# The second half of the receptance projection, ahead of the recurrence or beside it

## The chip, the cores and the metric

The kernel runs on one core of a Trainium2 chip. The metric is the device time of one execution in microseconds; of the kernel before three were timed.

## What is computed

Two layers of a causal decoder over 512 tokens of 1024 channels, and a final RMSNorm. Layer 0 is a mixture of windowed and differential attention, layer 1 is RWKV-7 time mixing; each is followed by a squared-ReLU MLP of width 4096. The change lies in layer 1, whose core is:

```python
xr, xw, xk, xv, xa, xg = [h + xx * mu[i] for i in range(6)]
r = xr @ w_r
k = xk @ w_k
v = xv @ w_v
...
def step(state, inp):
    r_t, w_t, k_t, v_t, a_t, b_t = inp
    sa = jnp.einsum('bhij,bhj->bhi', state, a_t)
    state = state * w_t[:, :, None, :] + sa[..., None] * b_t[:, :, None, :] + v_t[..., None] * k_t[:, :, None, :]
    return state, jnp.einsum('bhij,bhj->bhi', state, r_t)
```

r is 512 x 1024: 16 heads of 64 columns. It is read only in the recurrence and in the bonus term beside it.

## The kernel before, in words

Every float32 product is made of three products of a rounded part and a rest: weights and activations are split into hi and lo, and hi x hi, hi x lo, lo x hi are summed in PSUM (`mm3`, lines 175 to 178).

**Ahead of the recurrence** `rwkv_layer` (line 594) writes, in program order (lines 766 to 785): the k projection half 0, the decay path, k half 1, the a path, `xr = mix(0, 1)`, `project(W["w_r"], xr, 0, ...)`, then the gate path (`mix(5, 0)`, `g_weights`, `g_first`, `xv = mix(3, 0)`, `g_second`). `project` (line 709) makes 512 of the 1024 output columns with `gemm_group` (line 192): four chunks of weights, each 256 rows by 512 columns (512 KB). `wchunk` (line 162) loads one on the SP queue into `wraw` (three buffers, which the weights of the small paths use as well), ScalarE casts it to `whi` (line 167), VectorE subtracts it into `wlo` (line 169; two buffers each). With it TensorE does four token blocks x 2 row blocks x 3 matmuls of 512 columns into four PSUM banks. After the last chunk `spilled` (line 713) copies each bank by ScalarE (line 719) and sends it to the DRAM tensor `scr_r` on the ACT queue (line 605). The compiler's scheduler may move instructions of this stage past each other on an engine where their data allows.

**The recurrence** works on 16 units, each of 128 tokens and 4 heads (256 columns); units 0 to 7 are columns 0 to 511 (q = 0, 1), units 8 to 15 the others (q = 2, 3). A unit is a list of some hundred steps, each with a due time `AT[...]` counted in slots; unit n starts `PERIOD` = 8 slots after unit n - 1, so about four units are under way at once. All steps are sorted by due time and emitted in that order, and the `InOrder` wrapper (line 112) ties each engine's instructions to that order. What one unit takes is here called a period. A unit's score matmuls (`psc`, slot 7.0 and 7.1) are followed on VectorE by the masked scores `ms`, the rounding levels `lm`, and a chain of small float16 products (`p0` to `p14`) of which each needs a copy or sum (`e0` to `e14`) on ScalarE or VectorE before the next. Line 137 is the wrapper's, so all instructions of the recurrence carry it.

**Beside the recurrence** a generator, `side_work` (line 1438), fills TensorE with projections that have no place of their own: before the change v columns q = 0 and 1, r columns q = 2 and 3, v columns q = 2 and 3, and then parts of the output projection. `beside` (line 1370) makes 256 columns of 512 tokens in 16 pieces; a piece is 2 row blocks x 3 = 6 matmuls of 256 columns. `SIDE[n]` says how many pieces are spread evenly over period n. Their weights come in chunks of 512 rows by 256 columns (512 KB), cast in quarters by ScalarE and subtracted by GpSimd (lines 1352 and 1363). `evac_r` and `evac_v` copy the two finished banks and send them to DRAM on the ACT queue; `evac_v` also makes a mean-free copy on VectorE. Unit n loads its r at slot 8 n - 1.7 (line 874), and its v late, at 8 n + 18.8 (line 1158).

Of the kernel before, what the change touches and what calls it, by code (L numbers as in the profile page):

```python
# [10 lines left out]
F32 = mybir.dt.float32  # L11
# [7 lines left out]
P = 128  # L19
S = 512  # L20
# [49 lines left out]
FIRST = 8  # L70


SIDE = [16, 8, 9, 7, 8, 8, 9, 6, 11, 8, 6, 0, 8, 8, 6, 5, 8, 6, 7]
ORD = ['tensor', 'scalar', 'vector', 'gpsimd']
PERIOD = 8
PHASE = 0.5939277075075091
# [68 lines left out]
class Builder:  # L145
# [448 lines left out]
    def rwkv_layer(self):  # L594
        tc, nc, A = self.tc, self.nc, self.A
        W = {n: A["rwkv_" + n][0] for n in ("w_r", "w_k", "w_v", "w_o", "w0", "w1", "w2", "a0", "a1", "a2", "g1", "g2")}
# [7 lines left out]
        def spill(name, t, b, hf):  # L604
            nc.scalar.dma_start(scr[name][b * P:(b + 1) * P, hf * 512:(hf + 1) * 512], t)

        with ExitStack() as ctx:
# [20 lines left out]
            def mix(i, which, first=False, behind=None):  # L628
                xh, xl = self.xtiles(which)
                for k in range(KT):  # L630
                    if first:
                        nc.vector.scalar_tensor_tensor(self.h[k], self.h[k], self.g_mix[1][:, k:k + 1], rb,
                                                       op0=ALU.mult, op1=ALU.mult)
                        nc.vector.tensor_tensor(xx[k], self.hz[k][:, 1:S + 1], self.h[k], op=ALU.subtract)
                    t = lp.tile([P, S], F32, tag="mt", name=self.nm("mt"), bufs=3)
                    nc.vector.scalar_tensor_tensor(t, xx[k], mu[:, i, k:k + 1], self.h[k], op0=ALU.mult, op1=ALU.add)
                    if behind is not None and k >= XB:
                        with tc.issue_after(behind.ins):
                            nc.scalar.copy(xh[k], t)
                    else:  # L640
                        nc.scalar.copy(xh[k], t)  # L641
                    eng = nc.vector if not first and (XLA >> i & 1) and k % 2 else nc.gpsimd
                    eng.tensor_tensor(xl[k], t, xh[k], op=ALU.subtract)  # L643
                return xh, xl
# [57 lines left out]
            def wa_second(name, s, w):  # L702

                def mm(pb, bs, cs):
                    nc.tensor.matmul(pb, s[0][:, bs], w[1][0][:, cs], start=True, stop=False)
                    nc.tensor.matmul(pb, s[1][:, bs], w[1][1][:, cs], start=False, stop=True)
                blocks(spilled(name, AF.Tanh, 0.5), mm)

            def project(w, x, hf, evac, behind=None):
                self.gemm_group(w, 0, KT, hf * 512, *x, lambda m, ps: evac(m, hf, ps), token_major=True,  # L710
                                chunk=behind and (lambda *a: self.wchunk(*a, behind=behind)))

            def spilled(name, func=AF.Copy, scale=1.0):
                def evac(b, hf, ps):
                    t = lq.tile([P, 512], F32, tag="sp", name=self.nm("sp"), bufs=5)
                    if name == "g":
                        nc.vector.tensor_copy(t, ps)
                    else:
                        nc.scalar.activation(t, ps, func, scale=scale)
                    spill(name, t, b, hf)  # L720
                return evac
# [54 lines left out]
            xr = mix(0, 1)  # L776
            wa_second("a", sa, wa)
            project(W["w_r"], xr, 0, spilled("r"))
            xg = mix(5, 0)
            wg = g_weights()  # L780
            sg = g_first(xg, wg)
            xv = mix(3, 0, behind=self.gact)
# [7 lines left out]
            with ExitStack() as cx:  # L790
# [15 lines left out]
                def t2(name, pool_=wk, shape=(P, CW), dt=F32, bufs=None):  # L806
                    kw = {} if bufs is None else {"bufs": bufs}
                    return pool_.tile(list(shape), dt, tag=name, name=self.nm(name), **kw)
# [19 lines left out]
                nc = self.nc = InOrder(self, ORD)  # L828
# [3 lines left out]
                done = set()  # L832
# [24 lines left out]
                def unit(n):  # L857
                    b, q = units[n]
# [3 lines left out]
                    def at(name):  # L862
                        def add(f):
                            items.append((PERIOD * n + AT[name], f))
                            return f
                        return add


                    @at("load")
                    def _():  # L870
                        assert q < 2 or f"r{q}" in done
                        for t in ("w", "a", "k", "r"):
                            u[t] = t2("l" + t, ld)
                            nc.sync.dma_start(u[t], scr[t][rows, cs])
# [444 lines left out]
                def tokens(name, q, bk):  # L1319
                    return scr[name].rearrange("(m z p) c -> z p m c", z=2, p=P)[bk][:, :, q * CW:(q + 1) * CW]  # L1320

                def evac_r(q):
                    def evac(bk, ps):
                        t = self.tmp.tile([P, S], F32, tag="sq", name=self.nm("sq"))
                        nc.scalar.copy(t, ps)
                        nc.scalar.dma_start(tokens("r", q, bk), t.rearrange("p (m c) -> p m c", m=2))
                    return evac

                def evac_v(q):
                    def evac(bk, ps):  # L1330

# [38 lines left out]
                def beside(x, evac, name):  # L1370

                    pg = None
                    for kk in (0, 4):
                        wh, wl = taken()
                        if pg is None:
                            pg = [bank(p, name="side") for p in ps_g]
                        for m in range(4):
                            bk, ms = m % 2, slice(m * P, (m + 1) * P)
                            dst = pg[bk][:, (m // 2) * CW:(m // 2 + 1) * CW]
                            for k in range(4):  # L1380
                                xh, xl = x[0][kk + k][:, ms], x[1][kk + k][:, ms]
                                product(dst, [(xh, wh[:, k]), (xh, wl[:, k]), (xl, wh[:, k])], kk + k == 0 and m < 2, kk + k == 7)
                                if k % 2:
                                    if kk + k == 7 and m > 1:
                                        evac(bk, pg[bk])
                                        if m == 3:
                                            done.add(name)
                                    yield 0.5


                def project_o(cg, ks, ts, banks=None, last=True):
# [5 lines left out]
                    for k0 in ks:  # L1397
# [5 lines left out]
                        for m in range(4):  # L1403
# [12 lines left out]
                TH = S // 2  # L1416
                early, later = slice(0, TH), slice(TH, S)
                part_o = [None, None]
                order = [(W["w_v"], xv, evac_v, 0), (W["w_v"], xv, evac_v, 1), (W["w_r"], xr, evac_r, 2), (W["w_r"], xr, evac_r, 3),
                         (W["w_v"], xv, evac_v, 2), (W["w_v"], xv, evac_v, 3)]  # L1420
                first_o, whole_o = (0, 2), (0, 2, 4, 6)
                weights = chunks([(w, kk, 4, q * CW, CW) for w, x, e, q in order for kk in (0, 4)]
                                 + [(W["w_o"], k0, 2, cg * 512, 512) for ks in (first_o, whole_o) for cg in range(2) for k0 in ks]
# [3 lines left out]
                def taken():  # L1427
                    while not ready:
                        convert()
                    return ready.pop(0)  # L1430
# [6 lines left out]

                def side_work():
                    for w, x, e, q in order:
                        yield from beside(x, e(q), ("v" if e is evac_v else "r") + str(q))  # L1440
                    for cg in range(2):
                        yield from project_o(cg, first_o, later)
                    for cg in range(2):
                        yield from project_o(cg, whole_o, early)
# [10 lines left out]

                def outputs():

                    assert "v3" in done and "r3" in done and ("o", 7) in done
                    for l, x in zip((oh, ol), self.xtiles(0)):
                        l += x  # L1460
                    for k in range(KT // 2):
                        halves.append(self.xq.tile([P, S], F32, tag=f"xl{k}", name=self.nm("half")))
                        nc.sync.dma_start(halves[k], scr_o[k * P:(k + 1) * P, :])
                    self.h = [self.xq.tile([P, S], F32, tag=f"xh{k}", name=self.nm("h")) for k in range(KT)]
                    for k in range(KT):
                        nc.sync.dma_start(self.h[k], scr_h[k * P:(k + 1) * P, :])
# [9 lines left out]
                items = [i for n in range(NU) for i in unit(n)] + clears  # L1476
                for n, count in enumerate(SIDE):
                    items += [(PERIOD * (n + (i + PHASE) / count), beside_once) for i in range(count)]
# [8 lines left out]
            nc = self.nc = self.nc.nc  # L1487
# [99 lines left out]
```

## Time and profile before

| | us |
|---|---|
| three runs, median (lowest to highest) | 1526.73 (1521.74 to 1526.81) |
| profiled execution, whole | 1525.81 |
| its span, first to last instruction | 1523.9 |
| TensorE busy, share of the span | 1443.8, 95% |
| VectorE busy | 863.7, 57% |
| ScalarE busy | 684.2, 45% |
| GpSimd busy | 352.0, 23% |
| mean granted TensorE clock | 0.976 |

Layer 1's projections and gate lie at 650 to 793 us of the span, the recurrence with its side work at 793 to 1145, the rest of the output projection and the second MLP behind that. Busy shares are averages over stages with different limits. TensorE's matmuls are pipelined and the profile models their ends, so the time from one matmul's start to the next one's is less than the duration shown. A granted clock of 1.00 is 2.4 GHz; 0.50 is 1.2 GHz, and a figure in between is the mean of a stretch at both.

### The profile page before, as it was taken

The numbers are of one execution on the slowest core, as the hardware profiler recorded it, in microseconds if no ns is written. First come the engines' busy times: TensorE is split into PE (matmuls) and PEld (weight loads), VectorE is DVE, ScalarE is ACT, GpSimd is POOL, SyncE is SP. The second block draws the span as 40 slices with busy tenths as digits, with TensorE's granted clock in tenths as the row PEclk, the third lists the DMA queues.
The fourth block names the chain that finished last, engine by engine and source line by source line (L and its number), as shares of the span: only waits on it lengthen the run. The fifth ranks groups of instructions, "written<-read, shape, count | busy, mean of one in ns | idle before, by whom it ended". The sixth has DMA issues, their size and how long they took to land. (4 is left out here: it accounts for less than half of the span.)

```text
span 1523.9 us, 24386 instructions
## 1 busy us (share of the span) xinstructions
PE 1443.8 (95%) x9506; PEld 1172.4 (77%) x9506; DVE 863.7 (57%) x1491; ACT 684.2 (45%) x1394; POOL 352.0 (23%) x364
## 2 busy tenths in 40 slices
PE   7999999999999999969888999989998999999998
PEld 6765866878888888857667788868787888888887
DVE  5343565632335464497876778878866333354543
ACT  4245364432334343236634666666655233343533
POOL 4210200300000010052336455546655000000100
PEclk9999999999999999979989999989999999999999
DMA  5230310433333233324564345444223333333331
GB/s 193 80 90 1 96 57 27 102 104 85 97 97 97 97 124 98 102 64 152 176 192 147 116 139 154 127 143 119 64 95 118 90 97 97 97 97 97 97 97 70
DMA packets 117115, 159.76 MB, mean 105 GB/s; under 512 B 22524, under 2 KB 57892, under 8 KB 117000
## 3 DMA queue, kind: packets, MB, share of 16 engines
q1 hardware_dynamic: 103240, 140.37, 30.8%
q10 hardware_dynamic: 13760, 17.83, 3.5%
q8 instruction: 75, 1.23, 0.3%
q14 instruction: 40, 0.33, 0.1%
HBM read 133.00 MB, written 19.92 MB: 100 GB/s over the span
## 5 line engine op out<-in xcount | busy, mean ns | idle before, releaser
L169 DVE TENSOR_TENSOR wlo<-wraw,whi 128x1024 fp32r<-128x1024 f32 x172 | 219.9, 1280 | 263.1 <-ACT whi L167 263.0
L167 ACT CAST whi<-wraw 128x1024 fp32r<-128x1024 f32 x172 | 180.5, 1050 | 253.0 <-PE g L177 236.2
L176 PE MATMUL g<-xh,whi 128*128 128x512 f32 x640 | 250.2, 391 | 1.1 <-DVE Qa L442 1.1
L178 PE MATMUL g<-xh,wlo 128*128 128x512 f32 x640 | 249.0, 391 | 1.3 <-DVE wlo L169 1.1
L177 PE MATMUL g<-xl,whi 128*128 128x512 f32 x640 | 249.8, 390 | 0.0
L176 PE MATMUL g<-mh,whi 128*128 128x512 f32 x512 | 199.2, 389 | 0.0
L177 PE MATMUL g<-ml,whi 128*128 128x512 f32 x512 | 199.2, 389 | 0.0
L178 PE MATMUL g<-mh,wlo 128*128 128x512 f32 x512 | 199.2, 389 | 0.0
L316 POOL TENSOR_TENSOR acc<-acc,sq 128x512 f32<-128x512 f32 x29 | 48.8, 1683 | 636.4 <-issue 436.5
L184 DVE TENSOR_TENSOR ml<-m,mh 128x512 fp32r<-128x512 f32 x128 | 90.0, 706 | 148.9 <-ACT mh L183 148.8
L183 ACT CAST mh<-m 128x512 fp32r<-128x512 f32 x128 | 78.7, 616 | 191.3 <-PE g L178 191.1
L178 PEld LDWEIGHTS g<-xh,wlo 128*128 128x128 f32 x640 | 120.1, 188 | 28.3 <-DVE wlo L169 3.0
L176 PEld LDWEIGHTS g<-xh,whi 128*128 128x128 f32 x640 | 120.1, 188 | 27.2 <-DVE Qa L442 1.8
L177 PEld LDWEIGHTS g<-xl,whi 128*128 128x128 f32 x640 | 120.3, 188 | 24.7 <-issue 0.3
L178 PEld LDWEIGHTS g<-mh,wlo 128*128 128x128 f32 x512 | 96.1, 188 | 20.1
L176 PEld LDWEIGHTS g<-mh,whi 128*128 128x128 f32 x512 | 96.1, 188 | 20.1
L177 PEld LDWEIGHTS g<-ml,whi 128*128 128x128 f32 x512 | 96.1, 188 | 19.7
L137 POOL TENSOR_TENSOR wlo<-wraw,whi 128x256 fp32r<-128x256 f32 x100 | 76.6, 770 | 119.3 <-ACT whi L137 115.3
L177 PE MATMUL g<-wlo,xh 128*128 128x512 f32 x160 | 65.3, 408 | 4.5 <-DVE wlo L169 4.5
L176 PE MATMUL g<-whi,xh 128*128 128x512 f32 x160 | 63.0, 408 | 5.8 <-ACT xh L641 4.7
L643 POOL TENSOR_TENSOR xl<-mt,xh 128x512 fp32r<-128x512 f32 x28 | 47.5, 1712 | 86.9 <-ACT xh L641 73.5
L178 PE MATMUL g<-whi,xl 128*128 128x512 f32 x160 | 65.0, 406 | 0.6 <-POOL xl L643 0.5
(313 smaller groups left out, 2757.8 us busy)
## 6 DMA issues: line engine op xcount, KB each, us to landing
wraw<-in_mlp_w_dram SPq DMA_DIRECT2D x128, 512.0 KB
wraw<-in_attn_w_in_dram SPq DMA_DIRECT2D x24, 512.0 KB
wraw<-in_rwkv_w_o_dram SPq DMA_DIRECT2D x16, 512.0 KB
wraw<-in_attn_w_out_dram SPq DMA_DIRECT2D x8, 512.0 KB
wraw<-in_rwkv_w_k_dram SPq DMA_DIRECT2D x8, 512.0 KB
wraw<-in_rwkv_w_r_dram SPq DMA_DIRECT2D x8, 512.0 KB
wraw<-in_rwkv_w_v_dram SPq DMA_DIRECT2D x8, 512.0 KB
xt<-in_x_dram ACTq DMA_DIRECT2D x4, 512.0 KB
```

The costliest lines, as they stand in the source:

```text
L137: ins = op(*args, **kw)
L167: ins = [nc.scalar.copy(hi, raw)]
L169: ins.append((eng or nc.vector).tensor_tensor(lo, raw, hi, op=ALU.subtract))
L176: mm(ps, lh, rh, start=start, stop=False)
L177: mm(ps, lh, rl, start=False, stop=False)
L178: mm(ps, ll, rh, start=False, stop=stop)
L183: nc.scalar.copy(hi, src)
L184: nc.vector.tensor_tensor(lo, src, hi, op=ALU.subtract)
L316: nc.gpsimd.tensor_tensor(self.acc[0], self.acc[0], sq, op=ALU.add)
L643: eng.tensor_tensor(xl[k], t, xh[k], op=ALU.subtract)
```

## The change

The second half of r (columns 512 to 1023, 96 matmuls of 512 columns) is made by a second `project` call right behind the first, from the same `xr`. The two `beside` calls that made it (192 matmuls of 256 columns) leave the side work, and with them `evac_r`. `SIDE` gives the pieces that are left to the periods: periods 3 to 10 had 7, 8, 8, 9, 6, 11, 8, 6 and have 5, 4, 4, 4, 4, 4, 4, 2; all others keep their number. The v columns move up in the order.

```diff
-SIDE = [16, 8, 9, 7, 8, 8, 9, 6, 11, 8, 6, 0, 8, 8, 6, 5, 8, 6, 7]
+SIDE = [16, 8, 9, 5, 4, 4, 4, 4, 4, 4, 2, 0, 8, 8, 6, 5, 8, 6, 7]
@@ rwkv_layer
             project(W["w_r"], xr, 0, spilled("r"))
+            project(W["w_r"], xr, 1, spilled("r"))
             xg = mix(5, 0)
@@ unit, "load"
-                        assert q < 2 or f"r{q}" in done
@@
-                def evac_r(q):
-                    def evac(bk, ps):
-                        t = self.tmp.tile([P, S], F32, tag="sq", name=self.nm("sq"))
-                        nc.scalar.copy(t, ps)
-                        nc.scalar.dma_start(tokens("r", q, bk), t.rearrange("p (m c) -> p m c", m=2))
-                    return evac
@@
-                order = [(W["w_v"], xv, evac_v, 0), (W["w_v"], xv, evac_v, 1), (W["w_r"], xr, evac_r, 2), (W["w_r"], xr, evac_r, 3),
-                         (W["w_v"], xv, evac_v, 2), (W["w_v"], xv, evac_v, 3)]
+                order = [(W["w_v"], xv, evac_v, 0), (W["w_v"], xv, evac_v, 1), (W["w_v"], xv, evac_v, 2), (W["w_v"], xv, evac_v, 3)]
```

## Rows read from the trace of the kernel before

**Rows 1.** By stretch: length; busy PE, PEld, DVE, ACT, POOL (count); clock; DMA; GB/s.

```profile
740.00:774.00 34.00, 34.00 (x144) 26.94 (x143) 25.27 (x26) 20.32 (x36) 8.72 (x5) 0.96 0.71 209
774.00:793.00 19.00, 14.39 (x45) 9.49 (x44) 14.10 (x19) 6.71 (x13) 5.48 (x4) 0.73 0.39 115
...
844.10:999.20 155.10, 148.84 (x2086) 127.40 (x2082) 121.84 (x301) 97.89 (x279) 82.28 (x103) 1.00 0.46 135
```

**Rows 2.** VectorE's waits, 844.1 to 999.2: total us, times, longest.

```profile
DVE iu L137 <- PE prod L137: 18.8, 25, 1.7
```

**Rows 3.** TensorE in order of time, 748 to 765: start, duration, line, operands.

```profile
748.13 0.39 PE L176 MATMUL g<-whi,xh 128*128 128x512 f32 x1
...
765.07 0.39 PE L178 MATMUL g<-whi,xl 128*128 128x512 f32 x1
```

**Rows 4.** Groups by line, tile and form: count, busy us, mean ns, idle before.

```profile
L169 DVE TENSOR_TENSOR wlo<-wraw,whi 128x1024 fp32r<-128x1024 f32 x172 | 219.9, 1280 | 263.1 <-ACT whi L167 263.0
L167 ACT CAST whi<-wraw 128x1024 fp32r<-128x1024 f32 x172 | 180.5, 1050 | 253.0 <-PE g L177 236.2 <-PE g L178 11.1 <-issue 4.0
...
L137 POOL TENSOR_TENSOR wlo<-wraw,whi 128x256 fp32r<-128x256 f32 x100 | 76.6, 770 | 119.3 <-ACT whi L137 115.3 <-issue 1.4 <-POOL lw L137 1.2
...
L137 ACT CAST whi<-wraw 128x256 fp32r<-128x256 f32 x100 | 40.1, 405 | 6.4 <-DMA wraw<-in_rwkv_w_v_dram 3.6 <-PE side L137 2.0 <-DVE k_a L137 0.4
```

**Rows 5.** TensorE in order of time, gate path; in brackets its wait before.

```profile
785.75 0.80 PE L176 MATMUL l<-l2h,sgh 128*128 128x512 f32 x1 [2.79 <-DVE sp L717]
```

**Rows 6.** TensorE in order of time, a side piece and what follows it.

```profile
890.02 0.36 PE L137 MATMUL side<-whi,xh 128*128 128x256 f32 x1
...
890.81 0.28 PE L137 MATMUL prod<-m,id 128*128 128x256 f16 x1
```

**Rows 7.** VectorE and GpSimd in order of time, the update of the state.

```profile
931.82 0.78 DVE L137 TENSOR_TENSOR s<-st,pcf 128x128 f32<-128x128 f32 x1
938.07 0.29 DVE L137 TENSOR_TENSOR s<-st,pcf 128x128 f32<-128x128 f32 x1
...
931.71 0.74 POOL L137 TENSOR_TENSOR wlo<-wraw,whi 128x256 fp32r<-128x256 f32 x1 [0.59 <-ACT whi L137]
```

**Rows 8.** By stretch, instructions on the side tiles alone (PE, PEld, DVE, ACT).

```profile
844.10:999.20 155.10, 61.37 (x378) 49.38 (x378) 5.54 (x8) 4.39 (x8) 1.00 0.46 135
```

**Rows 9.** By period, from one unit's score matmuls to the next; columns of rows 1.

```profile
844.10:863.40 19.30, 17.54 (x245) 15.06 (x242) 14.03 (x34) 11.60 (x35) 8.97 (x12) 1.00 0.36 105
863.40:881.70 18.30, 18.16 (x256) 15.69 (x253) 14.30 (x36) 12.21 (x35) 10.24 (x13) 1.00 0.40 117
881.70:901.80 20.10, 19.02 (x270) 16.13 (x267) 14.43 (x38) 12.56 (x37) 10.59 (x14) 1.00 0.36 106
901.80:921.80 20.00, 19.63 (x277) 16.80 (x274) 14.86 (x40) 12.43 (x35) 10.22 (x13) 1.00 0.60 178
921.80:940.00 18.20, 17.28 (x259) 14.60 (x256) 14.98 (x36) 12.25 (x35) 10.49 (x14) 1.00 0.67 200
940.00:962.00 22.00, 21.31 (x292) 18.55 (x289) 18.32 (x43) 12.70 (x36) 11.24 (x15) 1.00 0.41 123
962.00:980.75 18.75, 18.55 (x268) 15.95 (x266) 15.13 (x40) 12.39 (x36) 11.05 (x14) 1.00 0.39 114
980.75:999.20 18.45, 17.36 (x260) 14.62 (x256) 15.79 (x41) 11.75 (x33) 9.49 (x12) 1.00 0.48 143
999.20:1020.20 21.00, 17.02 (x211) 13.35 (x208) 14.88 (x39) 11.53 (x33) 8.60 (x11) 0.76 0.59 169
1080.70:1099.10 18.40, 16.44 (x252) 13.84 (x249) 15.99 (x40) 12.20 (x37) 11.46 (x14) 1.00 0.23 66
```

**Rows 10.** VectorE in order of time, waits either side of 924.68 to 933.83.

```profile
924.68 0.42 DVE L137 TENSOR_TENSOR iu<-prod,int 128x256 f16<-128x256 f32 x1 [0.15 <-PE prod L137]
...
933.83 0.42 DVE L137 TENSOR_TENSOR iu<-prod,iu 128x256 f16<-128x256 f32 x1 [0.37 <-PE prod L137]
```

**Rows 11.** TensorE in order of time, ahead of the stretch at a lower clock.

```profile
1005.31 0.32 PE L137 MATMUL place<-iu,id 64*64 64x128 f16 x2 [2.46 <-DVE iu L137]
```

More of the change, by code (lines that the diff above doesn't have):

```diff
@@ L1439, in side_work @@
                     for w, x, e, q in order:
-                        yield from beside(x, e(q), ("v" if e is evac_v else "r") + str(q))
+                        yield from beside(x, e(q), f"v{q}")
                     for cg in range(2):
@@ L1456, in outputs @@
                 def outputs():
-                    assert "v3" in done and "r3" in done and ("o", 7) in done
+                    assert "v3" in done and ("o", 7) in done
                     for l, x in zip((oh, ol), self.xtiles(0)):
```

## The prediction, on record before the changed kernel ran

> **What bounds the kernel now.** I read the shares of the whole page first, then the busy time of each engine by stretch, then the same by period of the recurrence, and last single instructions. The profiled execution took 1525.81 us (span 1523.9 and 1.9 around it), 0.9 below the median of the runs, 1526.73; I work against the former and add 0.9 at the end. The change touches two stretches. In the first, 740 to 774, TensorE is busy 34.00 of 34.00 us [rows 1]: the first half of the receptance projection and the first gate matmuls run back to back, so work added there lengthens it by its own time. In the other, the eight periods of the recurrence from 844.1 to 999.2 out of which the change takes work, TensorE is busy 148.84 of 155.10 us and VectorE 121.84 [rows 1]. So TensorE is nearly the bound here too, but with VectorE not far behind: it has 33 us free, of which 18.8 are waits for one kind of TensorE product [rows 2]. The question is how much of the time taken out of these periods comes back before VectorE and the waits between the two take over.
>
> **What goes in.** Half 1 adds 8 row blocks x 4 token blocks x 3 = 96 matmuls of 512 columns. Half 0 issues the same back to back: from 748.13 to 765.07 there are 74 steps, 16.94 / 74 = 0.229 us each [rows 3]. 96 x 0.229 = **22.0 us**. By the Trainium skill, TensorE: Matmul & The Clock Gate, section Back-to-back issue gap, a step at full clock is the columns over 2.4 GHz and 2.5 ns, 0.216 us here, which an estimate would make 20.7 us; the row stands 6% above that, and it decides. With it come four weight loads of 512 KB on SP, four whi casts on ScalarE (1.05 us each), four wlo subtractions on VectorE (1.28), four copies out of PSUM on ScalarE and four spills on the ACT queue, all as half 0 has them [rows 4]. A chunk lasts 24 x 0.229 = 5.5 us on TensorE, so 1.65 to 1.9 us of ScalarE or VectorE work fits under it; VectorE has 8.7 us free in the 34, and needs 5.1 more in a stretch that grows by 22 [rows 1, 4]. I cost all of this at nothing; without cover, one late wlo would cost about its own 1.28 us per chunk, 5 us in all. On SP the four loads stand ahead of the gate weights and of the first weights of w_v. These wait for the same three raw buffers, so they come later by what TensorE comes later, and their users do too.
>
> Could it be less than 22? From 774 to 793 TensorE is busy 14.39 of 19.00 us at a granted clock of 0.73, for its gate products wait for VectorE's copies out of PSUM, up to 2.79 us [rows 1, 5]. If the scheduler set matmuls of half 1 into these gaps, up to 4.6 us would be hidden. Half 1 stands earlier in the program than the gate, and half 0, the nearest row, ran without a gap or a stranger in between [rows 3], so I take it as dense, and keep 17.4 as the lower end. An extra wait at the seam of the halves is bounded by the 1.28 above; the PSUM bank of block 0 has been emptied three blocks earlier.
>
> **What goes out.** Beside the recurrence the same half was 32 pieces of 6 matmuls of 256 columns. One piece holds TensorE from 890.02 to 890.81, **0.79 us** [rows 6]; 32 pieces are 25.3 us. Out go also 16 casts on ScalarE (0.405 us) and 16 subtractions on GpSimd (0.770) [rows 4], four copies and four spills, four SP loads; none of these engines ends the periods. The GpSimd part helps VectorE a little: an update of the state takes 0.78 us when a wlo of GpSimd runs and 0.29 when none does [rows 7]. 16 x 0.49 = 7.8 us is the most, and zero the least, as many fall on nothing; I leave it inside the period's price below.
>
> How much comes back is read from the periods, cut at the score matmuls. Their pieces by SIDE are 7, 8, 8, 9, 6, 11, 8, 6, sum 63, which the 378 side matmuls bear out [rows 8]; they become 5, 4, 4, 4, 4, 4, 4, 2. With 6 pieces a period takes 18.20 and 18.45, with 11 it takes 22.00 [rows 9]: 0.74 us a piece, close to the 0.79. But the five periods of 7 to 9 pieces average 19.29 at 8.0: from 8 to 6 the price is only 0.48. And the late period with 5 takes 18.40, no less than those with 6 [rows 9]. The free time of TensorE says why: 0.1 to 1.1 us at 8 pieces or more, 0.9 to 1.1 at 6, 2.0 at 5. From 924.68, just after the scores, to 933.83 VectorE waits for nothing [rows 10], and a piece there hides under it; only the pieces in the other half of the period, where VectorE waits for TensorE, are worth their time. So a period with 4 pieces lies between 18.3 (nothing more comes back) and 18.3 - 2 x 0.74 = 16.8. I take **17.4**, a little under 0.5 a piece: the rows at 8 to 6 are the nearest, the one at 5 is of a later unit with 15.99 us of VectorE work, where the early ones without a v column to finish have 14.0 to 15.1. The period that goes from 7 to 5: 19.3 - 1.0 = 18.3. The last goes from 6 to 2; the one behind it has a single piece, and there the clock falls to 0.76 and it takes 21.00 [rows 9]. The first of its slow matmuls follows a wait of 2.46 us [rows 11]. I leave that last period at 18.45.
>
> **Sum.** After: 18.3 + 6 x 17.4 + 18.45 = 141.15, against 155.10: 13.95 come back. 22.0 - 14.0 = **+8 us**, and 1526.73 + 8 = **1534.7**. What is late next in those periods is VectorE, at some 14.6 of 17.4 us, and the waits between it and TensorE. All behind the recurrence keeps its work and its order; unit 8's load of r, which needed side pieces of the periods before it, finds its data spilled long before. With 16.9 to 18.0 for the price the forecast's own range is 1531.5 to 1538.5.
>
> **Rivals.**
> *TensorE stays the bound down to four pieces.* Then each piece is worth its 0.79 and 25.3 us come back: 22.0 - 25.3 = -3.3, 1523.4, and with the gaps of 774 to 793 filled as well 1518.8: faster than before. It decides from 22.0 / 32 = 0.69 us a piece on. For it: TensorE's 148.84 of 155.10 and the 0.74 between 6 and 11 pieces. Against it: the 0.48 from 8 to 6 and the 18.40 at 5 [rows 9]. Chance 0.22 (0.08 of it with the gaps).
> *The clock falls.* With half the pieces TensorE waits more often, and in the period with one piece the granted clock was 0.76 [rows 9]. If that spreads, a period with 4 pieces lies halfway between 17.4 and 21.00, at 19.2; then 18.3 + 6 x 19.2 + 18.45 = 152 and 3 come back: +19, 1545.7. The Trainium skill, TensorE: Matmul & The Clock Gate, section Loop structure matters more than you think, says that waits between bursts of matmuls bring the half clock on; by that rule, this change makes such waits, and the row at one piece agrees. Against it: 1.00 in the period with 5 pieces, with 2.0 us free [rows 9]. Chance 0.18.
> *The added half isn't added in full:* the gaps before the recurrence take 4.6 us of it and the periods go as forecast: +3.4, 1530.1. Chance 0.10.
> The forecast has the other 0.50.
>
> **How the numbers follow.** About 0.5%, 7.6 us, is what a measurement of this kernel can tell from no change. The forecast lies just above it: of its 0.50, 0.32 are slower and 0.18 the same. The clock rival is slower (0.18). The third rival is the same (0.10), the first is the same without the gaps (0.14) and faster with them (0.08). So faster 0.08, same 0.42, slower 0.50. The range leaves out a little at both ends, 1520 to 1546.
>
> **What would show it.** In the profile after: 192 matmuls of w_r, not 96, ahead of the gate, at 0.229 us, the start of the recurrence (793) later by 20 to 23 us, and no new gap at the seam; side matmuls down by 192; periods of 4 pieces at 17 to 18 us with TensorE free some 2 us in each and VectorE near 0.85; a granted clock of 1.00 in them. Wrong if the start moves by under 18 (gaps filled), if those periods take 16.6 or less (TensorE bound), or over 18.5 with a clock under 0.95.

## The result, and the profile after

The changed kernel takes 1545.11 us (median, 1543.92 to 1546.51), beside 1526.55 for the kernel before on the same chip: a ratio of 1.0133 [1.0116, 1.0151], 18.6 us slower by the medians and 20.3 by the ratio. The forecast was slower too, by 8 us. The time lies in the range, but 10.4 us above the forecast of 1534.7 and 6.6 above its own upper end, 1538.5. Now and then an execution of any of these kernels takes some 30 us more at a lower granted clock; the times and ratios below leave these out.

The profiled execution has a span of 1543.1 us. These are its windows in the columns of [rows 1]: the stretch from 774, where the kernel before has its gate, now the later part of the added half and the first gate matmuls, then periods of the recurrence, cut at the score matmuls as in [rows 9], then eight periods in one row, and last the same stretch with the side tiles alone (PE, PEld, DVE, ACT).

```profile
774.00:795.70 21.70, 21.70 (x97) 17.44 (x96) 6.73 (x7) 10.53 (x18) 0.93 (x1) 1.00 0.86 256
...
865.81:884.49 18.68, 16.08 (x235) 13.61 (x232) 14.47 (x34) 11.45 (x34) 8.43 (x11) 1.00 0.36 110
901.63:918.74 17.11, 15.76 (x247) 13.20 (x244) 13.79 (x38) 10.99 (x32) 9.08 (x11) 1.00 0.28 79
918.74:945.75 27.01, 20.73 (x248) 17.18 (x244) 17.30 (x44) 12.35 (x35) 8.78 (x11) 0.75 0.37 112
945.75:962.81 17.06, 15.71 (x248) 13.20 (x244) 13.75 (x38) 11.08 (x33) 9.08 (x11) 1.00 0.52 121
...
997.26:1019.45 22.19, 16.97 (x242) 13.90 (x238) 15.56 (x40) 11.77 (x33) 8.37 (x11) 0.92 0.37 113
1019.45:1038.50 19.05, 15.50 (x206) 12.22 (x203) 14.54 (x40) 10.95 (x32) 8.36 (x11) 0.82 0.59 171
...
865.80:1019.45 153.65, 132.26 (x1902) 110.42 (x1897) 116.89 (x300) 90.73 (x260) 70.84 (x88) 0.94 0.37 104
...
865.80:1019.45 153.65, 33.05 (x192) 26.74 (x192) 6.41 (x10) 2.65 (x5) 0.94 0.37 104
```

And TensorE in order of time (start, duration, line, operands), one early in half 0 and the last of the added half:

```profile
748.02 0.40 PE L177 MATMUL g<-wlo,xh 128*128 128x512 f32 x1
...
787.40 0.39 PE L178 MATMUL g<-whi,xl 128*128 128x512 f32 x1
```

From the one to the other the trace has 172 steps, 0.229 us each, and no wait, also across the seam of the halves.

The ledger against the kernel before, by its own trace: the first score matmuls come at 830.6 us instead of 808.9, +21.7. The eight periods of [rows 1] take 153.65 instead of 155.10: only 1.45 comes back where 13.95 was forecast. The period behind them takes 19.05 instead of some 21, -2.0 (one finishing, described below, has moved out of it); the rest is within 1 us. That is the 19.2 us between the spans.

The rows say where the 12.5 missing us are. A plain period with four pieces takes 17.06 to 17.33 us at a granted clock of 1.00 (five of them), a little better than the 17.4 forecast; the one with five pieces takes 18.68 (forecast 18.3). Two periods spoil the sum: 27.01 and 22.19. They have no more side matmuls than the others, TensorE is free for 6.3 and 5.2 us in them instead of 1.35 in the two plain periods shown, and VectorE is busy 17.30 and 15.56 instead of 13.8. What they have and the others don't is the finishing of columns of v (`evac_v`, lines 1322 to 1334: ScalarE's copy `sq<-side`, then VectorE's `vm`, its scaling, and `vc<-side,vm`).

The order of time in the period of 27.01 shows it. Columns: start, duration, engine, line, operands, in brackets the wait before it and who ended it. First ScalarE and VectorE, then TensorE.

```profile
921.46 0.58 ACT L137 COPY sq<-side 128x512 f32<-128x512 f32 x1 [2.81 <-PE side L137]
924.53 0.40 ACT L137 CAST lt<-ms 64x256 f16<-64x256 f32 x1 [1.59 <-DVE ms L137]
932.16 0.59 ACT L137 COPY sq<-side 128x512 f32<-128x512 f32 x1 [1.29 <-PE side L137]
...
920.01 0.68 DVE L137 TENSOR_TENSOR ms<-psc,msk 128x512 f32<-128x512 f32 x1
922.07 0.69 DVE L137 TENSOR_REDUCE vm<-side 128x8 f32<-128x512 f32 x1 [1.39 <-ACT sq L137]
923.82 0.68 DVE L137 TENSOR_TENSOR ms<-psc,msk 128x512 f32<-128x512 f32 x1
932.78 0.69 DVE L137 TENSOR_REDUCE vm<-side 128x8 f32<-128x512 f32 x1 [2.22 <-ACT sq L137]
934.83 0.53 DVE L137 TENSOR_TENSOR s<-st,pcf 128x128 f32<-128x128 f32 x1
...
921.14 0.28 PE L137 MATMUL side<-whi,xl 128*128 128x256 f32 x1
924.88 0.25 PE L137 MATMUL place<-iu,id 64*64 64x128 f16 x2 [2.08 <-DVE iu L137]
935.51 0.70 PE L137 MATMUL pxs<-s,axs 128*64 128x64 f32 x8 [3.13 <-DVE s L137]
940.29 0.41 PE L137 MATMUL side<-wlo,xh 128*128 128x256 f32 x1
```

In the plain period that begins at 901.63 the same steps read:

```profile
902.98 1.35 DVE L137 TENSOR_TENSOR ms<-psc,msk 128x512 f32<-128x512 f32 x2
...
904.36 0.40 ACT L137 CAST lt<-ms 64x256 f16<-64x256 f32 x1 [0.22 <-DVE ms L137]
...
904.37 0.25 PE L137 MATMUL place<-iu,id 64*64 64x128 f16 x2
```

The 14th piece of a column quarter completes one PSUM bank, the 16th the other. The kernel writes the finishing directly behind these pieces, and `InOrder` keeps each engine's instructions in that order. With the new counts the 14th piece of the third quarter falls at 5.90 periods, just behind the score matmuls of a unit (at .88). TensorE runs it behind them and ends at 921.42. ScalarE's copy stands ahead of the casts `lt` and waits 2.81 us for it. VectorE's three mean steps stand between the two halves of `ms`, so the second half comes at 923.82, 5.1 us after the score matmuls instead of some 2. `place` starts 6.14 us after them instead of 2.74: 3.4 us late. The 16th piece, at 6.40, does it again to the state update: `vm` waits 2.22 us for ScalarE, `s` comes behind, and TensorE waits 3.13. After the waits the matmuls of 256 columns are recorded at 0.41 us instead of 0.28; the granted clock of the period is 0.75.

By the Trainium skill, Perfetto Trace Analysis, section Tensor Engine Instruction (MATMUL, LD_WEIGHTS), the queues of ScalarE, VectorE and GpSimd are strictly first in, first out. These rows agree: the second `ms` needed nothing that the mean steps make, and came behind them all the same.

In the kernel before the finishings of the third quarter stood at 8.60 and 8.78 periods, of the fourth at 10.60 and 10.93; in the changed one they stand at 5.90, 6.40, 9.90 and 10.80. That is the theory (A): the place of four finishings, not the pieces and not the added half, costs the missing time. The rival (B): the clock. With four pieces a period TensorE has so many pauses that the clock falls wherever something is added.

### The profile page after: what moved, and what is told of

The parts are those of the page before. It is cut to its first block, busy times and chain, and to the rows that moved or that the text cites. A ratio compares the mean times of both kernels' runs of the same rounds, so it can differ in the third digit from the quotient of the medians.

```text
span 1543.1 us, 24161 instructions
## 1 busy us (share of the span) xinstructions
PE 1448.1 (94%) x9410; PEld 1173.7 (76%) x9410; DVE 862.2 (56%) x1495; ACT 682.4 (44%) x1382; POOL 340.1 (22%) x348
## 5 line engine op out<-in xcount | busy, mean ns | idle before, releaser
L169 DVE TENSOR_TENSOR wlo<-wraw,whi 128x1024 fp32r<-128x1024 f32 x176 | 224.4, 1277 | 272.5 <-ACT whi L167 272.4
L167 ACT CAST whi<-wraw 128x1024 fp32r<-128x1024 f32 x176 | 184.7, 1050 | 262.6 <-PE g L177 238.0
L137 POOL TENSOR_TENSOR wlo<-wraw,whi 128x256 fp32r<-128x256 f32 x84 | 64.6, 774 | 110.6 <-ACT whi L137 98.2
L177 PE MATMUL g<-wlo,xh 128*128 128x512 f32 x192 | 78.0, 406 | 4.2 <-DVE wlo L169 4.2
L176 PE MATMUL g<-whi,xh 128*128 128x512 f32 x192 | 75.8, 407 | 5.8 <-ACT xh L641 4.7
L178 PE MATMUL g<-whi,xl 128*128 128x512 f32 x192 | 77.5, 404 | 0.6 <-POOL xl L643 0.5
```

The costliest lines, as they stand in the source:

```text
L137: ins = op(*args, **kw)
L167: ins = [nc.scalar.copy(hi, raw)]
L169: ins.append((eng or nc.vector).tensor_tensor(lo, raw, hi, op=ALU.subtract))
L176: mm(ps, lh, rh, start=start, stop=False)
L177: mm(ps, lh, rl, start=False, stop=False)
L178: mm(ps, ll, rh, start=False, stop=stop)
```

## Experiments

**The two parts of the change, each alone.** e1 is the kernel before with the added line; e2 is the changed kernel without it.

```
 e1 (on the kernel before)
             project(W["w_r"], xr, 0, spilled("r"))
+            project(W["w_r"], xr, 1, spilled("r"))
 e2 (on the changed kernel)
-            project(W["w_r"], xr, 1, spilled("r"))
                     spill(name, t, b, hf)
+                    if name == "r":
+                        spill(name, t, b, 1)
```

> The kernel before, with the second half of r made next to the first as well as beside the recurrence (it is written twice, with the same values): one part of the change alone. Theory A (the added half costs its full length, and what went wrong with the forecast lies in the recurrence): +22 us, 1548, the start of the recurrence later by 21 to 23, every period as before. Rival (half 1 disturbs more than its own length, through the buffers or the gate path): +26 or more, or periods 0 to 2 longer.

> The changed kernel without the added half, the other part alone: the first half's copies are sent to both halves of r's DRAM tensor, so the second half of r is left out of the computation. Theory A: the stall of the period 918.7 to 945.75 stands here too, since it comes from the order inside the recurrence; 1523, some 3 us below the kernel before and 22 below the changed one. Rival (the stall has to do with what the added half leaves in queues or in DMA): no stall, 1512 to 1514.

e1: 1550.44 us, ratio 1.0158 [1.0141, 1.0174], so +24.0; the score matmuls start at 830.88, 22.0 later. Not every period is as before: three early ones are 0.5 to 0.8 us longer, and in each TensorE waits 0.3 to 0.6 us for a small transfer, `kb<-la`, for which the kernel before has no such wait; it comes up again below. e2: 1528.73 us, ratio 1.0012 [0.9991, 1.0032], no gain at all; theory A's 1523 is missed by 5.7, since the two long periods are longer here than in the changed kernel. Its windows, a plain period and the two that finish v:

```profile
863.29:882.13 18.84, 15.40 (x231) 12.87 (x228) 13.55 (x36) 11.09 (x33) 8.89 (x11) 1.00 0.33 99
899.97:927.82 27.85, 21.89 (x247) 18.07 (x244) 17.28 (x44) 12.37 (x35) 8.79 (x11) 0.69 0.35 106
979.30:1004.43 25.13, 20.49 (x242) 16.78 (x238) 15.54 (x40) 11.79 (x33) 8.36 (x11) 0.73 0.34 103
```

Both long periods stand without the added half, so the rival that it causes them falls. The front is worth its forecast 22 us by itself, up to the start of the recurrence; the removal of 32 pieces gives nothing while the two long periods stand.

**The mean steps left out.** e3 is the changed kernel with VectorE's part of `evac_v` only for the first two quarters; for the other two the mean of v isn't made, and nothing is subtracted.

```
+                        if q < 2:
                             m = t2("vm", un, (P, 8))
                             nc.vector.tensor_reduce(m, hv(ps), axis=AX.X, op=ALU.add)
                             ...
```

> The changed kernel with VectorE's three instructions (mean, scale, difference) at the end of the last two v columns left out: the mean of v is not taken off there. Theory A (the 27 us period is made by these instructions, which stand in VectorE's fixed order right behind their last piece and make VectorE wait for it, and by the low clock that follows): that period falls from 27.05 to 17 to 18.5 at a clock of 1.00, the one of 22.2 to 18 to 20, the whole to 1531 to 1535. Theory B (four pieces in a period are too few to keep the clock up): the stall stays, 1542 to 1546.

1538.7 us, ratio 1.0079 [1.0063, 1.0095]. The answer lies between the two expectations: the long period falls from 27.01 to 21.50, not to 17, and the one of 22.19 only to 21.44. ScalarE in order of time shows what is left, its windows row stands below:

```profile
923.72 0.59 ACT L137 COPY sq<-side 128x512 f32<-128x512 f32 x1 [2.81 <-PE side L137]
...
925.32 0.83 ACT L137 CAST lt<-ms 64x256 f16<-64x256 f32 x2 [0.71 <-ACT whi L137]
...
921.00:942.50 21.50, 17.33 (x247) 14.70 (x244) 13.32 (x38) 12.09 (x35) 8.75 (x11) 0.92 0.45 138
```

The copy still waits for its piece in ScalarE's order, and the casts `lt` that the solve needs come 4.3 us after the score matmuls instead of 2.1. So leaving out VectorE's steps takes 5.5 of the 9.9 us off the first long period, with the clock back from 0.75 to 0.92, and 0.75 of the 5.1 off the second; the copy's place is in the rest.

**The pieces moved, so that both finishings stand elsewhere.** e4 places the four pieces that end the third quarter at 5.5 to 5.8 periods.

```
+                when = [n + (i + PHASE) / count for n, count in enumerate(SIDE) for i in range(count)]
+                for i, t in {45: 5.5, 46: 5.6, 47: 5.7, 48: 5.8}.items():
+                    when[i - 1] = t
+                items += [(PERIOD * t, beside_once) for t in when]
```

> The changed kernel with four pieces moved in time, none taken away: the last four of the third v column at 5.5, 5.6, 5.7 and 5.8 periods and not at 5.65, 5.90, 6.15 and 6.40, so that its two banks are finished where VectorE waits for TensorE anyway. Theory A (the place in the order makes the stall, not the amount of work): the 27 us period falls to 18 to 20, the whole to 1535 to 1538. Rival (the amount of VectorE's work, 3.5 us, makes it): the time only moves to another period, 1542 to 1546.

1542.32 us, ratio 1.0111 [1.0090, 1.0133]: a miss for theory A as I had put it. The finishing itself became cheap, since the period that now holds three more pieces and most of the finishing takes 19.86 us at full clock. But the next period, from which the pieces were taken, takes 21.39 at 0.68. The last two lines are of e6, which fills that gap again with pieces whose result nobody reads:

```
+                def filler():
+                    wh = kept[0]
+                    product(bank(ps_g[0], name="fill")[:, :CW], [(wh[:, k, :P], wh[:, k]) for k in (0, 1, 2, 3, 0, 1)], True, True)
+                items += [(PERIOD * t, filler) for t in (5.9, 6.15, 6.4)]
```

> The kernel of the run e4_place (the four pieces that end the third quarter of v moved up to 5.5 to 5.8 periods) with three filler pieces of six matmuls each, whose result nobody reads, at 5.90, 6.15 and 6.40 periods, where that run had no piece. All of the real work is done. If the low clock of that run's period of 21.39 us (0.68) came from TensorE having too little to do there, the period goes back to 17 to 17.6 us at 1.00 and the whole to 1539 to 1540 us. If it came from a wait in the solve chain that no piece can fill, the period stays at 21 or grows by the fillers, 1543 to 1545.

```profile
901.90:921.76 19.86, 18.30 (x266) 15.49 (x262) 15.77 (x41) 12.29 (x35) 10.07 (x13) 1.00 0.36 105
921.76:943.15 21.39, 18.68 (x228) 15.04 (x225) 14.84 (x40) 11.07 (x32) 7.88 (x10) 0.68 0.36 106
...
906.48:926.33 19.85, 18.29 (x265) 15.48 (x262) 15.80 (x42) 12.29 (x35) 10.05 (x13) 1.00 0.35 102
926.33:944.70 18.37, 16.00 (x247) 13.32 (x243) 15.42 (x40) 10.81 (x32) 7.87 (x10) 1.00 0.41 118
```

With the fillers that period is at 1.00 and takes 18.37, 3.0 us less with more work in it, if not the 17 to 17.6 expected: there the clock had a price. The whole didn't follow: 1544.86 us, ratio 1.0124 [1.0105, 1.0143]. In its profiled execution the recurrence starts 1.4 us later than in e4, its first period is 1.8 longer, a plain period runs at 0.91 (18.61 us, 17.12 at 1.00 in e4 with the same waits), and the stall of the fourth quarter, which neither kernel touches, is 23.88 instead of 21.79. So e6 reads one period, and no more.

**The finishing moved, the pieces left.** e5 and e8 write the finishing of the last two quarters later than its piece; e8 differs from e5 by the two times of the third quarter.

```
-                                        evac(bk, pg[bk])
+                                        if int(name[1]) >= 2 and name[0] == 'v':
+                                            pend.append((evac, bk, pg[bk]))
+                                        else:
+                                            evac(bk, pg[bk])
 ...
+                def finish():
+                    e, bk, ps = pend.pop(0)
+                    e(bk, ps)
+                items += [(PERIOD * t, finish) for t in (6.6, 6.64, 10.6, 11.2)]      # e5
+                items += [(PERIOD * t, finish) for t in (6.32, 6.62, 10.6, 11.2)]     # e8
```

> The changed kernel with the finishing of the last two quarters of v (ScalarE's copy, VectorE's three mean steps, the two stores) put into the engines' order later than the piece that ends each bank: at 6.60 and 6.64 periods instead of 5.90 and 6.40 for the third quarter, at 10.60 and 11.20 instead of 9.90 and 10.80 for the fourth. All pieces stay where they are and all work is done. Theory A (the stall is the finishing waiting for its own piece in front of the score and solve steps in the queues of ScalarE and VectorE, and the low clock follows from the stall): the period of 27.0 us becomes 18.5 to 19.5 at a clock of 1.00, the one of 22.2 becomes 18 to 20, so 1533 to 1537 us. Rival B (with four pieces a period TensorE's clock falls at any pause, wherever the finishing stands): the period stays above 21 us with a clock below 0.95, 1540 to 1545.

1540.57 us, ratio 1.0087 [1.0062, 1.0111]: by the whole that is B's range. The fourth quarter's period fell from 22.19 to 17.77, even below A's 18. The third quarter's stopped at 22.78 with a clock of 0.84, which is what B had said of it. VectorE in order of time gives the reason, which was my own edit:

```profile
935.85 0.69 DVE L137 TENSOR_TENSOR vc<-side,vm 128x512 f32<-128x512 f32 x1
...
940.02 0.69 DVE L137 TENSOR_TENSOR vc<-side,vm 128x512 f32<-128x512 f32 x1 [2.68 <-DMA scr_vc<-vc]
```

The tile `vc` has one buffer (line 1331), and with both finishings side by side the second waits for the store of the first, with the solve's steps queued behind it.

> As e5_late, but the two finishings of the third quarter of v lie 0.30 periods apart, at 6.32 and 6.62, since in e5_late the second vc waited 2.68 us for the store of the first (one buffer). The fourth quarter's stay at 10.60 and 11.20. All work is done. Theory A (the stall is only the finishing's place in the engines' order): that period falls from 22.78 to 18.3 to 19.3 us and the next from 18.50 to 17.1 at a clock of 1.00, the time from the first score matmuls to the last unit's from 279.6 to 273 to 275, so 1532 to 1535 us. Rival B (a period with 1.8 us of extra VectorE work and four pieces loses its clock): it stays above 21 us below 0.95, 1538 to 1541.

1532.60 us, ratio 1.0050 [1.0033, 1.0068]. Its windows: the period that finishes the third quarter, the one behind it, the fourth quarter's, the one without pieces, and the eight together.

```profile
918.74:937.52 18.78, 15.85 (x248) 13.24 (x244) 17.27 (x44) 12.18 (x35) 8.94 (x11) 1.00 0.48 150
937.52:954.56 17.04, 15.70 (x247) 13.20 (x244) 13.73 (x38) 11.09 (x33) 9.07 (x11) 1.00 0.51 133
989.00:1006.84 17.84, 15.18 (x242) 12.52 (x238) 15.62 (x41) 11.59 (x33) 9.78 (x12) 1.00 0.39 114
1006.84:1026.93 20.09, 17.50 (x207) 13.76 (x204) 14.79 (x39) 11.08 (x32) 7.32 (x10) 0.66 0.63 193
...
865.52:1006.84 141.32, 125.71 (x1901) 105.12 (x1897) 116.92 (x301) 90.56 (x260) 72.53 (x89) 1.00 0.38 110
```

This settles A against B. The same pieces at the same times, the same 17.3 us of VectorE work, and the period takes 18.78 us at a clock of 1.00 where it took 27.01 at 0.75. The order of four finishings is worth 18.6 - 6.5 = 12.1 us, each kernel against the one before in its own runs. The eight periods take 141.32 us: 13.8 come back. What is left of B is small: in the run that follows, the same period with the same waits of TensorE fell to a clock of 0.92 and took 1.4 us more.

**The recurrence part alone, without the stalls.** e9 is e2 with the finishings placed as in e8.

> The kernel of the run e2_gone (the change without the added 96 matmuls ahead of the recurrence, so the second half of r isn't computed; its stores write the first half's values) with the finishings placed as in e8_spaced. It measures what the removal of 32 pieces gives back when nothing stalls. Theory A: 14 to 16 us less than before, 1510 to 1513. If the pieces had been hidden beside other engines' work and only the stalls differ: 1518 to 1523.

1517.64 us, ratio 0.9946 [0.9926, 0.9966]: 8.5 us less. That misses A's 14 to 16 and lies at the edge of the other expectation. The eight periods take 143.35 us in this trace, so 11.75 come back there. One of them, the third quarter's, ran at a lower clock:

```profile
899.75:919.96 20.21, 17.28 (x248) 14.62 (x244) 17.27 (x44) 12.18 (x35) 8.93 (x11) 0.92 0.46 141
```

In e8 it has as many matmuls and the same recorded waits of TensorE, and takes 18.78: TensorE is busy 1.43 us longer here, and the period is 1.43 longer. The recurrence also starts 3.2 us later than in the kernel before, of which its first two periods take back 1.5. Part of the rest is a small transfer. TensorE's waits for it from 800 to 1130 us (columns: total, times, longest), in e9, then in e8:

```profile
PE tkb L137 <- DMA kb<-la: 3.0, 5, 0.8
...
PE tkb L137 <- DMA kb<-la: 0.4, 1, 0.4
```

The kernel before has no such wait in that stretch. Why the transfer lands later in some kernels, e1, e2 and e12 among them, stays open.

**The same wait in the kernel before.** There the second finishing of the fourth quarter stands at 10.93, also just behind the score matmuls. Its trace, ScalarE, and the row of [rows 11] is what follows on TensorE:

```profile
1001.88 0.59 ACT L137 COPY sq<-side 128x512 f32<-128x512 f32 x1 [2.81 <-PE side L137]
1004.96 0.41 ACT L137 CAST lt<-ms 64x256 f16<-64x256 f32 x1 [1.55 <-DVE ms L137]
```

It is the same 2.81 us. e10 moves the finishing of the fourth quarter to 10.62 and 11.20 in the kernel before; e7 leaves it and puts four filler pieces into that period (11.15, 11.40, 11.65, 11.85); e11 does both, and e12 puts the fillers into e8. The edits are those shown for e5 and e6, with these times.

> The kernel before with four filler pieces of six matmuls each, whose result nobody reads, at 11.15, 11.40, 11.65 and 11.85 periods, in the period that has no side pieces and ran 21.07 us at a clock of 0.76. All of the real work is done. If the clock is set by how little TensorE does there: that period falls to 17.2 to 18 us at 1.00 and the next from 21.40 (0.92) to 19 to 20, so 1521 to 1523 us. If the period is long for another reason (the loads of the second layer's tiles, the chain): no change or up to 3 us slower, 1527 to 1530.

> The kernel before with nothing but the finishing of the fourth quarter of v placed later, at 10.62 and 11.20 periods instead of 10.60 and 10.93. All work is done. In the kernel before, the copy at 1001.88 waits 2.81 us for its piece right behind the score matmuls, and the period takes 21.07 us at a clock of 0.76. Theory A (the same stall stands in the kernel before): that period falls to 17.5 to 18.5 us, 1522.5 to 1524 us, ratio 0.997 to 0.9985. Rival B (the period is long for want of pieces, at a low clock): no change, ratio 0.9995 to 1.001.

> The kernel of the run e10_before_late with the four filler pieces of e7_filler (six matmuls each, result read by nobody) at 11.15 to 11.85 periods. All work of the reference is done. In e7_filler the fillers raised the clock of that period from 0.76 to 0.92 and it stayed long (21.64 us), since the copy's wait stood in it; in e10_before_late the wait is gone and the period takes 19.66 us at 0.83. If what is left there is the clock, the period falls to 17.3 to 18.2 us at 1.00 and the whole to 1521 to 1522.5 us, ratio 0.996 to 0.9975. If it is the chain, it stays at 19.5 to 20.5, 1523 to 1524.5.

> The kernel of the run e8_spaced with the same four filler pieces, in its period that has no side piece (20.09 us at a clock of 0.66). If the clock makes it long: 17.3 to 18.2 us at 1.00, the whole 1530 to 1531.5. If the chain does: 19.5 to 20.5, 1532.5 to 1534.

The period in question, in the order e7, e10, e11, e12 (the kernel before has 21.00 at 0.76 in [rows 9], e8 has 20.09 at 0.66 above):

```profile
998.74:1020.38 21.64, 17.76 (x237) 14.87 (x234) 15.75 (x41) 11.88 (x33) 8.59 (x11) 0.92 0.55 170
...
996.67:1016.33 19.66, 16.08 (x213) 12.72 (x210) 15.11 (x39) 11.36 (x33) 8.61 (x11) 0.83 0.66 195
...
997.37:1017.07 19.70, 16.43 (x237) 13.75 (x234) 15.87 (x41) 11.76 (x33) 8.62 (x11) 1.00 0.64 198
...
1006.91:1027.33 20.42, 15.81 (x231) 13.12 (x228) 15.65 (x41) 11.49 (x32) 7.25 (x9) 1.00 0.60 173
```

e7: 1523.75 us, ratio 0.9999 [0.9985, 1.0013]: a higher clock and no shorter period. e10: 1523.15 us, ratio 0.9985 [0.9969, 1.0000]: the wait of 2.81 is gone from the trace, and so is the 2.46 on TensorE; the period is 1.4 us shorter, not the 2.5 to 3.5 that A expected. It has the lowest time of the kernels that compute everything, but its interval reaches no change, so a gain isn't shown. e11: 1523.86, ratio 0.9999 [0.9985, 1.0012]. e12: 1536.44, ratio 1.0076 [1.0056, 1.0096], above both expectations; TensorE's waits for `kb<-la` come to 3.7 us there, 0.4 in e8.

In e11 and e12 the fillers bring the clock to 1.00 and the period stays at 19.70 and 20.42. That looks as if the clock cost nothing, but two of the four fillers stand in the chain's way. The windows from the same matmul (`prod<-iu,hw`) to the next score matmuls in e10 and e11, and the two fillers in e11:

```profile
1010.99:1016.33 5.34, 5.34 (x70) 4.29 (x69) 2.01 (x7) 3.06 (x7) 1.41 (x2) 0.54 0.65 196
...
1011.73:1017.07 5.34, 4.97 (x83) 4.34 (x81) 2.80 (x8) 3.37 (x7) 1.42 (x2) 1.00 0.67 195
...
1011.85 0.96 PE L137 MATMUL fill<-whi 128*128 128x256 f32 x6
1016.28 0.96 PE L137 MATMUL fill<-whi 128*128 128x256 f32 x6
```

Both take 5.34 us, in e10 with TensorE busy all the time at a clock of 0.54. In e11 the two fillers hold it for 0.80 and 0.79 us, up to the start of the next matmul, so the rest of the matmuls, the same as in e10, took 3.75 us at 1.00. The clock gave back 1.6 us and the fillers took them. Without these two the period would be at some 18.1 us (an estimate, 19.70 - 1.59, which no run has), as the expectation for the clock had it. In e12 two fillers take as much, and a wait for `kb<-la` 1.27 us more. Of the second layer's tiles, which the other reading blames, the loads of `h` start at 902.5 to 925.2 us in the kernel before, far ahead of this period, and two of the four of `half` start in it; no run took those away, so their share isn't shown.

## Why the prediction was right or wrong, point by point

**Direction and range: right.** Slower had 0.50, and 1545.1 lies between 1520 and 1546. That it lies inside is luck: the upper end stands where it does for the clock rival's 1545.7, and what took the time there wasn't that rival.

**The part that goes in: right.** 172 steps at 0.229 us without a gap, the start of the recurrence later by 21.7 us in the changed kernel and 22.0 in e1, for a forecast of 22.0. Counted from the first `l<-l2h,ls` ahead of half 0 (738.52 in the kernel before), the start comes 91.0 to 93.0 us later in the eight traces with the added half and 68.4 to 70.4 in the kernel before, e7, e10 and e11: means 21.9 apart. The casts, loads and spills are hidden. The rival that the gaps before the recurrence take 4.6 us of it is out.

**The price of a period: right for what it counted.** 17.1 us for 17.4, at a clock of 1.00, TensorE free 1.35 us (the forecast said some 2), VectorE busy 13.8 (said 14.6). Without the stalls the eight periods take 141.32 us (e8) for 141.15, and the whole is 6.5 us over the before of its own runs (7.6 by the ratio) for a forecast of +8. A removed piece gives 13.8 / 32 = 0.43 us, not the 0.69 from which the change would pay, so the rival "TensorE stays the bound" is out too.

**The step that failed: "six periods at 17.4".** It priced a period by its count of pieces alone. The counts in SIDE also set when a column quarter is complete, and its finishing, 0.58 us of ScalarE and some 1.8 of VectorE a bank (in e8 17.27 - 13.73 = 3.54 for two), is written behind that piece. The part on what moves should have listed it: two banks from 8.60 and 8.78 to 5.90 and 6.40 periods, two from 10.60 and 10.93 to 9.90 and 10.80, each past the score, solve and state steps of its new place. The text set the work aside where it speaks of units "without a v column to finish" and never asked which of the new periods has one. [rows 9] had such a period: the one of 22.00, read as eleven pieces at 0.74 each, also holds both finishings of the third quarter (VectorE 18.32 us), so that price mixes the two. The place of the finishings is 12.1 us. The forecast missed by 10.4 and not by 12.1, mostly since the period behind the eight, left as it was in the text, came out 2.0 us shorter.

**A row was read and taken for something else.** The 2.46 us wait of [rows 11] and the 21.00 us at 0.76 were put down to a period with one piece. The wait follows the copy at 1001.88 that waits 2.81 us for that piece; without it (e10) the period is 1.4 us shorter, 19.66 at 0.83. Of what is left some 1.6 us is the clock's (e10 beside e11), so the reading was half right. Asking one step further back, what VectorE and ScalarE had in front of them, would have given the price of a finishing behind the score matmuls from the trace of before.

**The clock rival: its number came out by another cause.** It said 1545.7 with every period of four pieces at 19.2. In the trace five of them run at 1.00 in 17.1 to 17.3 us; within and behind the eight, the low clock stands in the two periods with a stall (0.75 and 0.92), in the one with no piece (0.82) and in the one behind it (0.92). The clock adds to a stall: matmuls at 0.41 instead of 0.28 us in the period of 27.01. Of its 9.9 us over a plain period TensorE is busy longer for 4.97, with the same matmuls, and free longer for 4.93; no run separated the clock from the stall any further. The rule of the Trainium skill that the prediction cited (TensorE: Matmul & The Clock Gate, Loop structure matters more than you think) fits the fall of the clock after these waits. Where two traces can be laid side by side the fall cost time: 3.0 us in one period (e4 against e6), 1.6 in another (e10 against e11), 1.4 in a third (e9 against e8).

## What to carry to other kernels

When a change alters how many slices of side work each period holds, list everything that fires on a count of them (a bank emptied, a mean, a store), and read what stands behind it in each engine's queue at the new place; the slices may be priced by their number, the finishing only by its place. If a finishing must go into an ordered queue, write it where its input has long been made and where no step of the chain stands behind it, and two that share a buffer a store apart. Before blaming a clock for a long period, follow the first wait in it one releaser further back. And a filler that is to hold the clock up is itself a slice with a place: where TensorE would have waited it is free, in front of the chain it takes what the clock gives.

## What the runs showed of the hardware that I had not expected

- The same period with the same waits of TensorE ran at two clocks: 18.78 us at 1.00 in e8 and 20.21 at 0.92 in e9, 17.12 at 1.00 in e4 and 18.61 at 0.91 in e6. TensorE waits for other engines in all four, and the lower clock cost 1.4 to 1.5 us all the same.
- A granted clock of 0.83 and one of 1.00 gave the same period, 19.66 and 19.70 us (e10, e11), only because the matmuls added to raise the clock took 1.6 us themselves.
- In a chain that goes through a small transfer from SBUF to SBUF (`kb<-la`, 64 KB), TensorE's waits for its landing were 0 us in the profiled execution of the kernel before, 0.4 in e8, 1.4 in e1, 3.0 in e9 and 3.7 in e12, though none of these kernels changes it.
- The start of the recurrence lies between 806.5 and 808.9 us in four kernels that are alike up to there (e10, e11, e7, the kernel before), and between 829.9 and 834.0 in the eight with the added half, so a difference of 2 us in one profiled execution says little.
